# Feed-forward up projections by Strassen's seven block products

## The chip, the cores and the metric

The kernel runs on one core of a Trainium2 chip. The metric is the device time of one execution in microseconds (us), here the median of three runs. TensorE multiplies matrices, VectorE and ScalarE work elementwise, GpSimd (POOL) does small elementwise work and issues DMAs of its own, SyncE (SP) issues the weight loads.

## The reference, cut to what matters

A decoder trunk of two residual layers on 512 tokens of 1024 features, all in float32. Layer 0 mixes by block-sparse attention and spatial gating, layer 1 by gated linear attention (GLA). Each layer then attends to 256 memory tokens and ends with a SwiGLU feed-forward of width 2816:

```python
def swiglu(h, w_gu, w_down):
    g, u = jnp.split(h @ w_gu, 2, axis=-1)
    return (jax.nn.silu(g) * u) @ w_down

x = x + swiglu(rmsnorm(x, norm_ffn[l]), ffn_w_gu[l], ffn_w_down[l])
```

`w_gu` is 1024 x 5632 (gate columns first, then up columns), `w_down` is 2816 x 1024.

## The kernel before, in words

The residual stream is kept transposed: `xT` has eight tiles of 128 features x 512 tokens. Every product is done in three matmuls: each operand is split into a high part, rounded to TensorE's float32r format, and a low part, the rest (`split`, lines 99 to 105: ScalarE copies the high part, VectorE subtracts it from the source). Then high x high, high x low and low x high are added up in one PSUM bank (`mm3`, lines 126 to 129).

Weights come from HBM through SP (`load_w`, line 115) into raw buffers (two), and are split into three pairs of buffers `wh`, `wl`. `ws_tile` (line 294) makes one tile of 128 output features x 512 tokens with weights as the stationary operand. `gemm_as` (line 303) holds activations stationary and makes tiles of 128 tokens x 512 columns (matmul lines 314 to 316).

The pre-norm is folded in: `prep` (line 262) multiplies a finished tile of `xT` by the norm's gain while it splits it, and adds its squares to `acc`. `finish` (line 275) sums `acc` over the partitions on TensorE, takes the inverse root on POOL, and `rb_of` (line 231) spreads the per-token column to a row on all partitions by two matmuls. The row is applied to the products when they leave PSUM.

The feed-forward (line 885 on) works in three parts of 8, 8 and 6 hidden tiles. `ffn_hidden` makes the gate tile, scales it and applies silu, makes the up tile, scales it, multiplies both, and splits the result. The down projection of the part follows: `ws_tile` in layer 0 (`ffn_mid`), `gemm_as` in layer 1 (`ffn_last`). The tiles that feed it are made just before, in `out_last` (line 444), the last half of the cross attention's output projection, which calls `prep` for each finished tile.

SBUF beside the weights is a set of 61 slots of 128 x 512 (`Slots`, line 46; the one freed longest ago is handed out first), and small pools of their own for the softmax rows (`pp`), their transposes (`pt`), and scratch (`tj`, `em`, `es`, `acc`). PSUM has eight banks: four `m`, two `s`, two `t`.

The order of instructions on each engine is made by the framework when the program is built: among the instructions that a model of their times holds to be ready, the one that stands first in the program goes first. So an engine can take up later work while earlier work waits. On the chip each engine then runs its list strictly in that order.

Of the kernel before, what the change touches and what calls it, by code (L numbers as in the profile page):

```python
# [18 lines left out]
P = 128  # L19
# [26 lines left out]
class Slots:  # L46
    """[128, 512] fp32 slots of SBUF handed out in program order, oldest freed first."""
# [19 lines left out]
def trunk(ctx: ExitStack, tc: tile.TileContext, io, out):  # L67
# [9 lines left out]
    xp = ctx.enter_context(tc.tile_pool(name="chain", bufs=1))  # L77
# [3 lines left out]
    # ---------------------------------------------------------------- helpers  # L81
# [24 lines left out]

    def chain(tag, bufs, dtype=F32):
        return xp.tile([P, T], dtype, tag=tag, name=tag, bufs=bufs)
# [45 lines left out]
    # ---------------------------------------------------------- early loads  # L154
# [38 lines left out]
    # parameter columns  # L193
# [11 lines left out]
    # -------------------------------------------------------- x: transposes  # L205
# [25 lines left out]
    def rb_of(rcol):  # L231
        """the per-token column [128, 4] as a row on every partition [128, 512]"""
# [13 lines left out]
    def col_sums(ps, src):  # L246
        """ps[:, t] = the sums over the partitions of src's 128-token blocks"""
# [14 lines left out]
    def prep(nm, m, gcol):  # L262
        """feature tile m of the next sub-layer's input, and its part of the sum of squares"""
        h, l = split_slots(xT[m], gcol)
        nm.h.append(h)
        nm.l.append(l)
        if m == 0:
            nm.acc = tp.tile([P, T], F32, tag="acc", name="acc", bufs=1)
# [6 lines left out]
    def finish(nm):  # L275
        ps = ps_t()
        col_sums(ps, nm.acc)
        nm.rcol = rsqrt_cols(ps[:, :NT], NT, 1.0 / D)
        nm.rb = rb_of(nm.rcol)

    def new_norm():
        nm = Norm()
        nm.h, nm.l = [], []
        return nm
# [5 lines left out]
    # ------------------------------------------------------------- GEMM forms  # L290
# [3 lines left out]
    def ws_tile(wv, c0, bh, bl, k0=0):  # L294
        """one [128 features, 512 tokens] tile: weights stationary"""
# [7 lines left out]
    def gemm_as(load, ah, al, ntok, evac):  # L303
        """ntok x [128 tokens, 512 columns]: activations stationary"""
# [20 lines left out]
    # ------------------------------------------------------- memory projections  # L325
    def mem_prep(l):
        """gained and transposed memory tokens in two parts, and their norms to be applied later"""
        mh, ml, rss = [], [], []
        ss = [small(2), small(2)]
        for hf in range(2):  # L330
            r = [chain("pp", NPP), chain("pp", NPP)]
            for mt in range(2):
                nc.sync.dma_start(r[mt], io["mem"][0, mt * P:(mt + 1) * P, hf * T:(hf + 1) * T])
            for mt in range(2):
                j = tmp(tag="tj", bufs=1)
                A.activation(j, r[mt], AF.Square, accum_out=ss[mt][:, hf:hf + 1])
            for k2 in range(2):
# [11 lines left out]
                ml.append(l_)  # L349
        for mt in range(2):  # L350
# [9 lines left out]
    def kv_proj(l, mh, ml, rss):  # L360
        """keys and values of the memory; yields between its four products"""
# [7 lines left out]
        def keys(half):  # L369
            kn = [None, None]  # L370

            def evac_k(mt, ps):
                kn[mt] = sl.get()
                ss = small(2)
                for hh in range(2):
                    j = tmp(tag="tj", bufs=1)
                    A.activation(j[:, :MEM], ps[:, hh * MEM:(hh + 1) * MEM], AF.Square,
                                 accum_out=ss[:, hh:hh + 1])
                r = rsqrt_cols(ss, 2, rss[mt][1])
# [64 lines left out]
    def out_last(w, k0, ch, cl, nm, gname, l):  # L444
        """the last part, and the next sub-layer's input"""
        out_part(w, k0, ch, cl, lambda m: prep(nm, m, pcol(gname, l * KD + m)))
        finish(nm)
# [800 lines left out]
```

## Time and profile before

| | |
|---|---|
| runs (three) | median 1523.46 us, 1522.89 to 1526.95 |
| profiled execution, span | 1523.4 us |
| granted TensorE clock, mean | 0.999 |
| instructions | 18140 |
| HBM read, written | 139.88 MB, 2.10 MB |

The profile's span runs from the first to the last instruction of the profiled execution; the page gives no other time for it, and the span differs from the median of the runs by 0.06 us. In the timeline each row has a start, a duration and the instruction; matmuls overlap, so their rate is read from starts. "L128" is line 128 of the kernel before.

### The profile page before, as it was taken

To read this page: it belongs to the slowest core of one execution; us is meant where nothing else is said; L and a number is where in the kernel's file an instruction comes from. 1 tells how busy PE (TensorE), PEld (TensorE's weight loads), DVE (VectorE), ACT (ScalarE), POOL (GpSimd) and SP (SyncE) were. 2 spreads that over 40 slices of the span, in tenths; PEclk is the share of its full clock that TensorE was granted. 3 is DMA by queue.
4 is the path that set the end of the run, shared out by engine and by line. 5 is a ranking of instruction groups with operands and counts; after the bars stand their busy time and mean duration, and the time that the engine had idled before them with its cause. 6 is when DMAs were issued, how large, how long until landed. Compare 5 with 4: busy or idle time off the path is not lost.

```text
span 1523.4 us, 18140 instructions
## 1 busy us (share of the span) xinstructions
PE 1508.1 (99%) x7050; PEld 1241.8 (82%) x7050; DVE 863.9 (57%) x1451; ACT 620.2 (41%) x1014; POOL 83.3 (5%) x104
## 2 busy tenths in 40 slices
PE   8999999999999999999999999999999999999998
PEld 6787778888888888888787887888888888888887
DVE  6876875755654344344667565776557443443443
ACT  6546663643532133222454443555435332332231
POOL 4511100000000000000000000100000000000000
PEclk9999999999999999999999999999999999999999
DMA  7231432312333333333323222253123322332332
GB/s 216 83 97 56 125 102 65 97 56 97 94 89 95 102 98 94 101 95 95 103 64 97 70 69 71 94 159 93 58 68 97 97 92 91 97 95 97 97 98 95
DMA packets 197606, 143.15 MB, mean 94 GB/s; under 512 B 6093, under 2 KB 176193, under 8 KB 197521
## 3 DMA queue, kind: packets, MB, share of 16 engines
q1 hardware_dynamic: 195616, 140.53, 30.4%
q0 software_dynamic: 800, 1.37, 0.4%
q8 instruction: 55, 0.90, 0.2%
q10 hardware_dynamic: 1104, 0.11, 0.1%
q14 instruction: 31, 0.25, 0.0%
HBM read 139.88 MB, written 2.10 MB: 93 GB/s over the span
## 4 chain that ended last, share of the span: by engine, by line
PE 93%; DVE 2%; ACT 1%; POOL 1%; issue 0%; ACTq 0%; POOLq 0%
PE ps_mm L129 21%; PE ps_mm L128 21%; PE ps_mm L127 21%; PE ps_mm L314 6%; PE ps_mm L316 6%; PE ps_mm L315 6%; PE ps_t L132 2%; PE ps_s L127 1%; PE ps_t L127 1%; PE ps_t L128 1%; PE ps_t L129 1%; PE ps_s L129 1%; PE ps_s L128 1%; PE ps_s L585 1%; DVE wl L102 0%; PE ps_s L249 0%
## 5 line engine op out<-in xcount | busy, mean ns | idle before, releaser
L128 PE MATMUL ps_mm<-slot,wh 128*128 128x512 f32 x1424 | 555.9, 391 | 0.0
L129 PE MATMUL ps_mm<-slot,wl 128*128 128x512 f32 x1424 | 555.3, 391 | 0.0
L127 PE MATMUL ps_mm<-slot,wh 128*128 128x512 f32 x1424 | 552.7, 390 | 0.5 <-DVE slot L105 0.5
L101 ACT ACTIVATE wh<-raw 128x1024 fp32r<-128x1024 f32 (+1 forms) x258 | 271.6, 1053 | 631.9 <-PE ps_mm L128 469.3
L102 DVE TENSOR_TENSOR wl<-raw,wh 128x1024 fp32r<-128x1024 f32 (+1 forms) x258 | 314.1, 1218 | 161.3 <-ACT wh L101 155.0
L129 PEld LDWEIGHTS ps_mm<-slot,wl 128*128 128x128 f32 x1424 | 267.5, 188 | 55.4 <-DVE wl L102 0.2
L127 PEld LDWEIGHTS ps_mm<-slot,wh 128*128 128x128 f32 x1424 | 267.4, 188 | 55.4 <-DVE slot L105 0.6
L128 PEld LDWEIGHTS ps_mm<-slot,wh 128*128 128x128 f32 x1424 | 267.5, 188 | 54.8
L314 PE MATMUL ps_mm<-wh,slot 128*128 128x512 f32 x496 | 195.1, 396 | 1.4 <-DVE slot L711 1.4
L315 PE MATMUL ps_mm<-wh,slot 128*128 128x512 f32 x496 | 195.3, 394 | 0.0
L316 PE MATMUL ps_mm<-wl,slot 128*128 128x512 f32 x496 | 189.7, 392 | 0.0
L314 PEld LDWEIGHTS ps_mm<-wh,slot 128*128 128x128 f32 x496 | 93.7, 189 | 20.5 <-DVE slot L711 1.8
L315 PEld LDWEIGHTS ps_mm<-wh,slot 128*128 128x128 f32 x496 | 93.7, 189 | 18.3
L316 PEld LDWEIGHTS ps_mm<-wl,slot 128*128 128x128 f32 x496 | 93.2, 188 | 18.7
L898 DVE TENSOR_TENSOR tmp<-ps_mm,rb 128x512 f32<-128x512 f32 x44 | 30.4, 691 | 132.9 <-PE ps_mm L129 132.7
L139 POOL TENSOR_TENSOR s<-s,mhalf 128x2 f32<-128x2 f32 (+3 forms) x46 | 50.9, 1110 | 640.7 <-DVE s L137 636.5
L894 DVE TENSOR_TENSOR tmp<-ps_mm,rb 128x512 f32<-128x512 f32 x44 | 30.4, 691 | 94.0 <-PE ps_mm L129 90.7
L440 DVE TENSOR_TENSOR slot<-ps_mm,slot 128x512 f32<-128x512 f32 x64 | 43.5, 687 | 29.5 <-PE ps_mm L129 29.3
L914 DVE TENSOR_TENSOR slot<-ps_mm,slot 128x512 f32<-128x512 f32 x24 | 16.5, 690 | 56.9 <-PE ps_mm L129 56.9
L101 ACT ACTIVATE slot<-tmp 128x512 fp32r<-128x512 f32 x48 | 30.3, 632 | 32.6 <-DVE tmp L899 28.2
L102 DVE TENSOR_TENSOR slot<-tmp,slot 128x512 fp32r<-128x512 f32 x48 | 32.9, 685 | 2.3 <-ACT slot L101 2.1
L899 DVE TENSOR_TENSOR tmp<-tmp 128x512 f32<-128x512 f32 x44 | 30.4, 692 | 4.4 <-ACT wh L101 0.5
(285 smaller groups left out, 1362.4 us busy)
## 6 DMA issues: line engine op xcount, KB each, us to landing
raw<-in_ffn_w_gu SPq DMA_DIRECT2D x88, 512.0 KB, 3.9
raw<-in_ffn_w_down SPq DMA_DIRECT2D x38, 512.0 KB, 3.6
raw<-in_xa_w_kv SPq DMA_DIRECT2D x32, 512.0 KB, 3.8
raw<-in_od_w_in SPq DMA_DIRECT2D x24, 512.0 KB, 3.7
raw<-in_xa_w_q SPq DMA_DIRECT2D x16, 512.0 KB, 3.8
raw<-in_xa_w_out SPq DMA_DIRECT2D x16, 512.0 KB, 3.5
raw<-in_ev_w_in SPq DMA_DIRECT2D x12, 512.0 KB, 4.6
raw<-in_ev_w_in SPq DMA_DIRECT2D x16, 256.0 KB, 2.9
```

The lines of the kernel that those rows point to most:

```text
L101: A.activation(h, src, AF.Copy)
L102: V.tensor_tensor(l, src, h.bitcast(F32), ALU.subtract)
L127: PE.matmul(ps, ah, bh, start=start, stop=False)
L128: PE.matmul(ps, ah, bl, start=False, stop=False)
L129: PE.matmul(ps, al, bh, start=False, stop=stop)
L132: PE.transpose(ps, src, ident)
L139: G.tensor_tensor(r, m, mhalf[:, :n], ALU.pow)
L314: PE.matmul(pss[t], a, wh[:, kk, :], start=st, stop=False)
L315: PE.matmul(pss[t], b, wh[:, kk, :], start=False, stop=False)
L316: PE.matmul(pss[t], a, wl[:, kk, :], start=False, stop=sp_)
L440: V.tensor_tensor(xT[m], ps, xT[m], ALU.add)
L894: V.tensor_tensor(g, ps, nm.rb, ALU.mult)
```

## The change

Both operands of the up projection are cut in two along each side: tokens into halves of 256, features into even and odd tiles, columns into gate and up columns. The four block products of the result (gate and up, for each token half) are then made from seven block products in place of eight, by Winograd's form of Strassen's scheme.

- Activations: `prep7` scales a tile of `xT` by the gain on ScalarE, without a split; for each pair of tiles `blocks7` makes the four sums S1 to S4 of quarter blocks on VectorE and splits three tiles (and a fourth for each second pair).
- Weights: four products take raw blocks (A11, A12, S4, S3; for S3 one raw block is first added to another on VectorE), three take sums that are built up in slots by DMAs that add to SBUF, issued by POOL (`accum_op=ALU.add`).
- Products: activations stationary, tokens on the output's partitions, blocks of 256, then five times 512 columns of each of gate and up. Partial sums stay in PSUM where the scheme allows it, and are copied out in between.
- The norm is now a per-partition scale at the evacuation, so the row `rb` isn't made for the feed-forward norms.
- The hidden tiles, tokens on partitions, are turned by TensorE transposes (`turn`), run as `tick`s between the next block's products, and then split. The down projection takes 6, 8 and 8 tiles.
- `pp`, `pt`, `tj`, `em`, `es`, `acc` come from the slots, now 72; raw buffers are four in place of two.

The diff, cut to its core:

```diff
+    def prep7(nm, m, gcol):
+        y = sl.get((P, 2, MEM))
+        yf = y.rearrange("p a b -> p (a b)")
+        A.activation(yf, xT[m], AF.Copy, scale=gcol)
+        nm.y.append(y)
+        sum_squares(nm, m)
+        if len(nm.y) == 2:
+            blocks7(nm, *nm.y)
+            nm.y = []
+    def blocks7(nm, y0, y1):
+        first = len(nm.ops) % 2 == 0
+        e = sl.get((P, 2, MEM))
+        V.tensor_tensor(e[:, 0, :], y0[:, 1, :], y1[:, 1, :], ALU.subtract)
+        V.tensor_tensor(e[:, 1, :], e[:, 0, :], y0[:, 0, :], ALU.subtract)
+        if first:
+            nm.e4 = sl.get((P, 2, MEM))
+        V.tensor_tensor(nm.e4[:, 0 if first else 1, :], y1[:, 0, :], e[:, 1, :], ALU.add)
+        V.tensor_tensor(y0[:, 1, :], y0[:, 0, :], y0[:, 1, :], ALU.subtract)
+        h, l = [], []
+        for src in (y0, y1, e):
...
+            split(h[-1], l[-1], src)
...
+        if not first:
...
+            split(h4, l4, nm.e4)
...
-    def finish(nm):
+    def finish(nm, row=True):
...
-        nm.rb = rb_of(nm.rcol)
+        if row:
+            nm.rb = rb_of(nm.rcol)
...
+    def mm7(wv, c0, c1, w, ops, sink, tick):
...
+        for p in range(n2):
+            q.append([sl.get(), sl.get()])
+            for i in range(2):
+                k = 4 * p + 2 * i
+                nc.sync.dma_start(q[p][i][:, 0:w], wv[:, k, c1:c1 + w])
+                nc.gpsimd.dma_start(q[p][i][:, 0:w], wv[:, k, c0:c0 + w], accum_op=ALU.add)
+        pa_, pc_, pb_ = [[banks[g]() for _ in range(2)] for g in "mst"]
...
+        def chain_sum(kh=None, c=None):
+            def get(p):
+                h, l = new_hl()
+                for i in range(2):
+                    split(h[:, i, 0:w], l[:, i, 0:w], q[p][i][:, 0:w])
+                    if kh is not None:
+                        nc.gpsimd.dma_start(q[p][i][:, 0:w], wv[:, 4 * p + kh + 2 * i, c:c + w],
+                                            accum_op=ALU.add)
...
+        def steps(acc, first, get, name, end):
+            for p in range(n2):
+                h, l = get(p)
+                tick()
+                for i in range(2):
+                    oh, ol, j = ops[2 * p + i][name]
+                    st, sp_ = first and p == 0 and i == 0, p == n2 - 1 and i == 1
+                    for t in range(2):
+                        o = acc[t][:, 0:w]
+                        ah, al = oh[:, j, t * P:(t + 1) * P], ol[:, j, t * P:(t + 1) * P]
+                        PE.matmul(o, ah, h[:, i, 0:w], start=st, stop=False, skip_group_check=True)
+                        PE.matmul(o, al, h[:, i, 0:w], start=False, stop=False, skip_group_check=True)
+                        PE.matmul(o, ah, l[:, i, 0:w], start=False, stop=sp_, skip_group_check=True)
+                        if sp_:
+                            sink(end, t, o)
+                yield
...
+        product(pa_, True, raw_block(0, c0), "A11", "m")
+        product(pc_, True, chain_sum(1, c1), "S1", "q")
+        product(pb_, True, raw_block(1, c0), "A12", "b")
+        product(pa_, False, chain_sum(1, c0), "S2", "u")
+        for _ in zip(steps(pc_, False, b22, "S4", "c"), steps(pa_, False, t3, "S3", "v")):
+            pass
+        product(pa_, False, chain_sum(), "A22", "a")
...
-    parts_ff = [(0, 8), (8, 16), (16, 22)]
...
+    blocks_ff = [(0, 2), (2, 6), (6, 10), (10, 14), (14, 18), (18, 22)]
+    rounds_ff = {1: (0, 1), 3: (2, 3), 5: (4, 5)}
...
+            def sink(what, t, ps):
+                if what in ("m", "q", "u"):
+                    x = sl.get()
+                    {"m": M, "q": Q, "u": U}[what][t] = x
+                    A.activation(x[:, :w], ps, AF.Copy)
+                elif what == "b":
+                    V.tensor_tensor(M[t][:, :w], M[t][:, :w], ps, ALU.add)
+                    A.activation(M[t][:, :w], M[t][:, :w], AF.Silu, scale=nm.rcol[:, t:t + 1])
+                elif what == "c":
+                    V.tensor_tensor(U[t][:, :w], ps, U[t][:, :w], ALU.subtract)
+                    scaled(U[t][:, :w], U[t][:, :w], t, M[t][:, :w])
+                    sl.free(M[t])
+                elif what == "v":
+                    V.tensor_tensor(Q[t][:, :w], Q[t][:, :w], ps, ALU.subtract)
+                else:
+                    g = sl.get()
+                    A.activation(g[:, :w], ps, AF.Silu, scale=nm.rcol[:, 2 + t:3 + t])
+                    scaled(Q[t][:, :w], Q[t][:, :w], 2 + t, g[:, :w])
+                    sl.free(g)
...
+            def turn(j):
+                def go():
+                    ps = ps_t()
+                    for t in range(NT):
+                        transpose(ps[:, t * P:(t + 1) * P], hid[t][:, (j - j0) * P:(j - j0 + 1) * P])
+                    self.gh[j], self.gl[j] = split_slots(ps)
...
+        def rounds(self):
+            for b in range(len(blocks_ff)):
+                self.up(b)
+                if b - 1 in rounds_ff:
+                    yield self.round(*rounds_ff[b - 1])
+            sl.free(*self.nm.slots)
+            self.flush()
+            yield self.round(*rounds_ff[len(blocks_ff) - 1])
...
-NSLOTS = 61
-NPP = 4
-NPT = 7
+NSLOTS = 72
 TMP = 3
-NRAW = 2
+NRAW = 4
```

## Rows read from the trace of the kernel before

**Rows 1.** The page: busy time by engine; TensorE's granted clock in 40 slices, tenths.

```profile
PE 1508.1 (99%) x7050; PEld 1241.8 (82%) x7050; DVE 863.9 (57%) x1451; ACT 620.2 (41%) x1014; POOL 83.3 (5%) x104
...
PEclk9999999999999999999999999999999999999999
```

**Rows 2.** The page: the chain that ended last, share of the span by engine.

```profile
PE 93%; DVE 2%; ACT 1%; POOL 1%; issue 0%; ACTq 0%; POOLq 0%
```

**Rows 3.** Waits of TensorE: who for whom, us in total, times, longest.

```profile
PE ps_mm L132 <- DMA slot<-in_x: 6.0, 2, 3.5
...
PE ps_mm L127 <- DVE slot L105: 0.5, 1, 0.5
```

**Rows 4.** Timeline of TensorE (start us, duration us, instruction): two neighbours of 512 columns.

```profile
240.16 0.39 PE L128 MATMUL ps_mm<-slot,wh 128*128 128x512 f32 x1
240.38 0.39 PE L129 MATMUL ps_mm<-slot,wl 128*128 128x512 f32 x1
```

**Rows 5.** Timeline of TensorE: two neighbours of 256 columns.

```profile
337.19 0.28 PE L127 MATMUL ps_s<-slot,slot 128*128 128x256 f32 x1
337.31 0.28 PE L128 MATMUL ps_s<-slot,slot 128*128 128x256 f32 x1
```

**Rows 6.** Transposes: timeline of TensorE, and a group (count, busy us, mean ns).

```profile
1178.49 1.04 PE L132 MATMUL ps_t<-ident,slot 128*128 128x128 f32 x8
1179.28 0.48 PE L127 MATMUL ps_mm<-slot,wh 128*128 128x512 f32 x1
1179.60 0.40 PE L128 MATMUL ps_mm<-slot,wh 128*128 128x512 f32 x1
...
L132 PE MATMUL ps_t<-ident,slot 128*128 128x128 f32 x96 | 16.5, 284 | 0.0
```

**Rows 7.** Groups by line and shape: count, busy us, mean ns, idle before.

```profile
L102 DVE TENSOR_TENSOR wl<-raw,wh 128x1024 fp32r<-128x1024 f32 x250 | 306.6, 1226 | 160.2 <-ACT wh L101 153.9 <-PE ps_mm L128 5.6
L101 ACT ACTIVATE wh<-raw 128x1024 fp32r<-128x1024 f32 x250 | 264.9, 1060 | 613.7 <-PE ps_mm L128 453.1 <-PE ps_mm L315 111.2 <-issue 21.7
L102 DVE TENSOR_TENSOR slot<-tmp,slot 128x512 fp32r<-128x512 f32 x48 | 32.9, 685 | 2.3 <-ACT slot L101 2.1
L101 ACT ACTIVATE slot<-tmp 128x512 fp32r<-128x512 f32 x48 | 30.3, 632 | 32.6 <-DVE tmp L899 28.2 <-DVE tmp L733 4.4
L102 DVE TENSOR_TENSOR sL<-st,sH 128x256 fp32r<-128x256 f32 x28 | 11.7, 421 | 5.8 <-ACT sH L101 5.4 <-PE ps_s L129 0.2
```

**Rows 8.** Timeline of VectorE in layer 0's last half of the attention's output projection.

```profile
383.08 1.29 DVE L440 TENSOR_TENSOR slot<-ps_mm,slot 128x512 f32<-128x512 f32 x2 [5.02 <-PE ps_mm L129]
...
397.18 0.69 DVE L440 TENSOR_TENSOR slot<-ps_mm,slot 128x512 f32<-128x512 f32 x1
...
400.17 0.69 DVE L273 TENSOR_TENSOR acc<-acc,tmp 128x512 f32<-128x512 f32 x1
400.78 0.75 DVE L105 SCALAR_TENSOR_TENSOR slot<-slot,pc,slot 128x512 fp32r<-128x512 f32 x1
401.44 0.69 DVE L273 TENSOR_TENSOR acc<-acc,tmp 128x512 f32<-128x512 f32 x1
```

**Rows 9.** Windows: length, busy by engine (instructions), granted clock, DMA share, GB/s.

```profile
0.00:38.00 38.00, 30.52 (x134) 25.22 (x135) 24.67 (x77) 23.67 (x50) 15.48 (x33) 1.00 0.72 216
...
382.00:404.00 22.00, 22.00 (x99) 18.23 (x98) 19.02 (x27) 13.21 (x20) 0.00 (x0) 1.00 0.33 96
...
420.00:460.00 40.00, 40.00 (x178) 33.12 (x177) 21.08 (x26) 14.18 (x18) 0.00 (x0) 1.00 0.32 92
...
960.00:963.40 3.40, 3.40 (x16) 2.95 (x17) 1.63 (x4) 0.49 (x2) 0.00 (x0) 0.51 0.02 8
```

**Rows 10.** DMA issues: tile, queue, count, KB each, median us to landing.

```profile
raw<-in_ev_w_in SPq DMA_DIRECT2D x16, 256.0 KB, 2.9
...
slot<-in_ev_w_s POOLq DMA_DIRECT2D x2, 256.0 KB, 6.6
```

**Rows 11.** Timeline of POOL: one issue of a DMA of 256 KB.

```profile
13.10 0.56 POOL L653 DMA_DIRECT2D slot<-in_ev_ln_g  x1
```

More of the change, by code (lines that the diff above doesn't have):

```diff
@@ L283, in new_norm @@
         nm.h, nm.l = [], []
+        nm.y, nm.ops, nm.slots = [], [], []
         return nm
@@ L323, in as_loader, with block, load, new_hl @@
         return load
+    def mm7(wv, c0, c1, w, ops, sink, tick):
+        n2 = len(ops) // 2
+        def block(kh, c, p):
+            return wv[:, 4 * p + kh:4 * p + kh + 3:2, c:c + w]
+        def load(kh, c, p):
+            raw = wp.tile([P, 2, T], F32, tag="raw", name="raw", bufs=NRAW)
+            nc.sync.dma_start(raw[:, :, 0:w], block(kh, c, p))
+            return raw
+        def new_hl():
+            return (wp.tile([P, 2, T], F32R, tag="wh", name="wh", bufs=NWH),
+                    wp.tile([P, 2, T], F32R, tag="wl", name="wl", bufs=NWL))
+        q = []
+        for p in range(n2):
[5 more added lines that the diff above has]
+        pa_, pc_, pb_ = [[banks[g]() for _ in range(2)] for g in "mst"]
+        def raw_block(kh, c):
+            def get(p):
+                raw = load(kh, c, p)
+                h, l = new_hl()
+                split(h[:, :, 0:w], l[:, :, 0:w], raw[:, :, 0:w])
+                return h, l
+            return get
+        def chain_sum(kh=None, c=None):
+            def get(p):
+                h, l = new_hl()
+                for i in range(2):
[3 more added lines that the diff above has]
+                                            accum_op=ALU.add)
+                if kh is None:
+                    sl.free(*q[p])
+                return h, l
+            return get
+        def t3(p):
+            r = load(0, c1, p)
+            V.tensor_tensor(r[:, :, 0:w], r[:, :, 0:w], r22[p][:, :, 0:w], ALU.add)
+            h, l = new_hl()
+            split(h[:, :, 0:w], l[:, :, 0:w], r[:, :, 0:w])
+            return h, l
+        r22 = {}
+        def b22(p):
+            r22[p] = load(1, c1, p)
+            h, l = new_hl()
+            split(h[:, :, 0:w], l[:, :, 0:w], r22[p][:, :, 0:w])
+            return h, l
+        def steps(acc, first, get, name, end):
+            for p in range(n2):
+                h, l = get(p)
+                tick()
+                for i in range(2):
+                    oh, ol, j = ops[2 * p + i][name]
[9 more added lines that the diff above has]
+                yield
+        def product(*args):
+            for _ in steps(*args):
+                pass
[4 more added lines that the diff above has]
+        for _ in zip(steps(pc_, False, b22, "S4", "c"), steps(pa_, False, t3, "S3", "v")):
+            pass
+        product(pa_, False, chain_sum(), "A22", "a")
@@ L330, in mem_prep @@
         for hf in range(2):
[L331 removed]
+            r = [sl.get(), sl.get()]
             for mt in range(2):
@@ L349, in mem_prep @@
                 ml.append(l_)
+            sl.free(*r)
         for mt in range(2):
@@ L442, in out_part, with out_last @@
                     done(m)
-    def out_last(w, k0, ch, cl, nm, gname, l):
-        out_part(w, k0, ch, cl, lambda m: prep(nm, m, pcol(gname, l * KD + m)))
-        finish(nm)
+    def out_last(w, k0, ch, cl, nm, gname, l, seven=False):
+        make = prep7 if seven else prep
+        out_part(w, k0, ch, cl, lambda m: make(nm, m, pcol(gname, l * KD + m)))
+        finish(nm, not seven)
     wv = wview(io["ev_w_in"][0])
@@ L627, in moba_pair @@
             split(oH, oL, osum)
+            sl.free(osum)
             sl.free(qH, qL, kH, kL)
@@ L864, in cross @@
                 ptl.append(l_)
+            sl.free(*pts)
             for dv in range(2):
@@ L872, in cross @@
                 oL.append(l_)
+            sl.free(*pth)
+            sl.free(*ptl)
         sl.free(*kh)
@@ L923, in ffn_last @@
         xk = None
-        for pi, (j0, j1) in enumerate(parts_ff):
-            gh, gl = ffn_hidden(l, nm, j0, j1)
-            last = pi == len(parts_ff) - 1
-            if last:
-                free_norm(nm)
+        for j0, gh, gl, last in Ffn(l, nm).rounds():
             if xk is None:
@@ L1070, in gla_qk @@
         ksH, ksL = split_slots(ps)
+        sl.free(em, es)
         hs[hd] = ep, qpH, qpL, kiH, kiL, ksH, ksL
```

97 lines of the change are left out of this document (61 added, 36 removed).

## The prediction, made before the changed kernel ran

> **What bounds the kernel now.** I read the busy shares first: TensorE is busy 99% of a span of 1523.4 us and its clock is at full level in every slice [rows 1]. The chain of waits agrees: 93% of it is TensorE [rows 2]. The list of TensorE's waits shows that it hardly waits behind its first loads: the input transposes wait 6.0 us for x, and no product on the feature tiles of a norm loses more than 0.5 us to VectorE, over the whole run [rows 3]. So the time is a count of TensorE instructions times their spacing, and everything else is cover. The spacing is read from starts, not from the durations, which overlap: matmuls of 512 columns start 0.227 us apart [rows 4], of 256 columns 0.120 us apart [rows 5]. The profile's span (1523.4) and the median of the runs (1523.46) differ by 0.06 us, so the sum below is made against 1523.4 and holds for both.
>
> **The up projections.** Before, each layer makes 44 tiles of 8 x 3 matmuls of 512 columns: 1056 x 0.2267 = 239.4 us. After, a block makes 7 products, each of 4 feature tiles x 2 token halves x 3 = 24 matmuls: 168. Five blocks are 512 wide, 5 x 168 x 0.2267 = 190.4 us, one is 256 wide, 168 x 0.120 = 20.2 us. Per layer 28.8 us go, for both **-57.6 us**. It is the pattern of the activations-stationary loops, whose neighbours have the same spacing, so I take no range on it.
>
> **The turns.** The output stands with tokens on partitions and must be turned: 22 x 4 = 88 transposes a layer, 176 in all. Eight of them in the trace hold TensorE from 1178.49 to 1179.28 us, 0.10 each, and the matmul behind them starts its successor 0.09 late [rows 6]. A group of four is then about 0.46 us (0.35 to 0.5), 44 groups: **+20.2 us** (15 to 22). The Trainium skill speaks against this edit (TensorE: Matmul & The Clock Gate, Part 4: PE-mode transpose): it puts a 128x128 transpose inside a kernel at some 275 ns. Rows 6 have that number as the mean duration (284 ns), but not as the spacing; by the page the edit would cost 48 us, by the spacing 20 us. I sum with the spacing.
>
> **The row of norms.** The feed-forward norms no longer spread rcol to a row: two 512-column matmuls in each layer go, **-0.9 us**; the ScalarE and VectorE steps of that row lay beside TensorE anyway.
>
> **The start of the feed-forward.** This is the price I expect to see most. While TensorE makes the last half of the attention's output projection, VectorE already runs without a gap from 383.08 to 402.1 us [rows 8], 19.0 us busy in 22 [rows 9]. TensorE's own last tile there was ready at 397.2, its split for the norm at 401.5; TensorE bridged that without a wait, since the feed-forward's first output tiles need it last. After, VectorE loses eight scaled subtractions (start to start 0.66: 5.3 us) and gains 16 half-size differences (0.42 us each, back to back some 0.34: 5.4 us) and 14 split halves of 128x512 (0.69, back to back 0.60: 8.4 us) [rows 7, 8]. So its work ends 8.5 us later, at about 410.6; the first product needs all but the last three splits, 408.8. TensorE can put in between only what needs feature tiles 0 to 3 and has weight buffers (three pairs): the first half of the products A11 and S1 in the narrow block, 24 x 0.120 = 2.9 us, and 0.8 us of column sums. Idle: 408.8 - 397.2 - 3.7 = 7.9 us. After idle time the trace shows the clock at its lower level (1.2 GHz, granted 0.51) for 3.4 us [rows 9], which takes half of that again, 1.7 us. 9.6 us a layer: **+19.2 us**. Ends: 6 us if the scheduler slips the weight splits and more half-products into the gaps, 28 us if VectorE takes everything in program order and the ScalarE halves add waits.
>
> **Inside a block.** Per wide block TensorE has 38.1 + 1.8 = 39.9 us. VectorE has eight 128x1024 splits (1.23), two additions of that size, twelve 128x512 splits (0.69), ten evacuation steps and four splits of turned tiles (0.69): 30.2 us, 76%; ScalarE 8 x 1.06 + 22 x 0.63 + the silus = 25 us [rows 7]. Before it was 21.1 us in 40 [rows 9]. That fits on average, with three weight buffer pairs of 2.7 us each ahead. One wait has no cover: the subtraction of the S3 partial sum (label v) reads the bank on which A22, the very next product, accumulates. The first bank is read 0.69 us while the second bank's last three matmuls run (0.68); the pipeline's end (0.39 - 0.23 = 0.16) and the semaphores leave 0.3 us bare. When VectorE is just in another instruction (it is 70% of the time, half of 0.7 to 1.2 us left) another 0.3 comes on top. 0.6 x 12 blocks: **+7.2 us**, between 0 (next block's matmuls fill it) and 24 (each time a whole 1.23 us split and a second one stand before). What is queued behind: the c steps and A22's own splits, all with slack of one product, 5.4 us.
>
> **The narrow block** gives every wait half the cover: **+2 us** for both layers, from 0 to 6.
>
> **The summing DMAs.** T sums are made by DMAs that add to SBUF, 12 a block, issued by POOL (0.56 us each, and POOL has nothing else there) [rows 11]. None is in the trace. The nearest row is a plain 256 KB load from POOL, 6.6 us to landing in the crowded start, against 2.9 us from SP [rows 10]. The slack: S1's first split can begin when its buffer is freed, at A11's start; it is done 2.3 us later, the DMA goes out, and S2 wants its own split to begin 14.3 us after A11's start (six half-products of 2.72, less 2.0): 12 us. At 3 to 6.6 us it is hidden, also if reading the destination makes it half as long again: +0, between 0 and 48 (landing in 16 us). Bytes: a wide block moves 8.4 MB in 39.9 us, 210 GB/s; the first 38 us of the kernel moved 216 GB/s at a DMA share of 0.72 [rows 9]. SP's loads will therefore land later than now, but four raw buffers instead of two cover that: 0.
>
> **Pooled buffers.** Attention and GLA take their scratch from the common slots. Counted through, at least ten slots are free at the tightest place of the feed-forward, and a slot comes back several products after it was freed: 0, between -3 and +3 (these stages lose little to waits now, and could gain or lose it).
>
> **Sum.** -57.6 + 20.2 - 0.9 + 19.2 + 7.2 + 2 = -9.9: 1523.4 - 9.9 = **1513.5 us**.
>
> **The rivals.** Without any wait the arithmetic alone gives 1523.4 - 38.3 = 1485.1 us.
> (a) The preparation is hidden and the v wait filled: 1485.1 + 3 = 1488. For it: the order of work already fills such places (0.5 us of waiting at most at the old starts). Against: VectorE's work there exceeds TensorE's, and no order makes it less. 0.18.
> (b) The start costs its upper end, 28 us: 1522. 0.12.
> (c) VectorE's order inside the blocks fails: 2 us a block and 6 for the narrow ones, 1485.1 + 19.2 + 24 + 6 = 1534. Speaking for it: peaks, since in A22's 5.4 us VectorE has 6.9 us; against: three buffers ahead. 0.10.
> (d) The slower side: the adding DMA lands late. S2's split waits for it, TensorE stands at S2 in every block. From 12 us of landing on each further us costs 10 us over the wide blocks, so from about 13 us the change is a loss; at 16 us, 4 us x 12 = 48: 1561. For it: 6.6 us for a plain one, and this one reads its target too; against: that row is from the crowded start. 0.12.
> (e) The transposes cost their duration, not their spacing: 176 x 0.284 = 50 us instead of 20.2: 1543. The page named above would have it so. Rows 6 speak against it. 0.04.
> My forecast has 0.44.
>
> **How the numbers follow.** A measurement of this kernel tells about 0.3%, 4.6 us, from no change: below 1518.9 is faster, above 1528.0 slower. Faster: (a) and nearly all of the forecast, 0.60. Same: (b) and the edges, 0.16. Slower: (c), (d) and (e), less an edge, 0.24. The range leaves out half of (d) and (e) above and the tail of (a): 1486 to 1538; the forecast's own range is 1503 to 1524.
>
> **What would show it.** TensorE idle of some 8 us with the clock halved behind it at both feed-forward starts, released by VectorE splits of prep; 2016 up matmuls with unchanged spacing; groups of four transposes at 0.4 to 0.5 us; a wait of 0.3 to 1 us on the v subtraction once a block; adding DMAs landing in under 8 us and no TensorE wait behind them. I am wrong if the starts cost under 3 us each, if the blocks are spaced above 42 us, or if the S2 splits wait for DMA.

## The result, and the profile after

The changed kernel takes 1576.08 us (median of 4 runs, 1567.11 to 1580.58), the kernel before, beside it, 1523.18 (1522.29 to 1526.95): ratio 1.0328, 95% interval [1.0293, 1.0363]. It is slower by 53 us where I said 10 faster, and outside the range. The profiled execution has a span of 1578.9 us, 55.5 more than before. In each run here an execution's time is some 1.7 us longer than its span (1580.58 and 1578.9), so the 0.06 us between span and median before was chance.

The page of the changed kernel: busy time, tenths in 40 slices, DMA queues (packets, MB, share of 16 engines) and the chain by engine.

```profile
PE 1510.9 (96%) x7126; PEld 1237.6 (78%) x7126; DVE 974.0 (62%) x1651; ACT 737.8 (47%) x1258; POOL 211.0 (13%) x248
...
PEclk9999889999999999999999999999999999999999
DMA  8222313313579378436322212263146774773351
...
q1 hardware_dynamic: 137120, 152.07, 30.6%
q0 software_dynamic: 21536, 35.98, 14.0%
...
PE 83%; DVE 4%; DMA 4%; ACT 3%; issue 1%; POOL 1%; DVEq 0%; ACTq 0%; POOLq 0%
```

The count of instructions is the predicted one: 7050 [rows 1] - 96 up matmuls - 4 of the norm rows + 176 transposes = 7126. But TensorE's part of the chain fell from 93% [rows 2] to 83%, and DMA, VectorE and ScalarE have taken the rest. The DMA line reaches 9 tenths in the first feed-forward and 7 in the second.

TensorE's waits, longest first (the same view as [rows 3]: us in total, times, longest), and VectorE's longest wait for a DMA.

```profile
PE ps_t L443 <- DVE slot L101: 17.4, 4, 7.6
PE ps_mm L443 <- ACT wh L100: 9.9, 8, 3.2
PE ps_mm L128 <- DMA slot<-in_x: 5.4, 2, 3.6
PE ps_s L444 <- DVE slot L101: 5.1, 2, 2.7
PE ps_mm L444 <- DVE slot L101: 4.6, 2, 2.3
```

```profile
DVE raw L420 <- DMA raw<-in_ffn_w_gu: 54.0, 18, 7.8
```

L443 to L445 are the three matmuls of a product, L101 is the low half of a split, L420 the addition that makes S3's weight sum. ps_t is the pair of PSUM banks that A12's product and the turned hidden tiles use in turn. The place of the longest wait, in layer 0, on the chain (start us, us; the first line, a group of four transposes, is used further down), on VectorE's timeline, on TensorE's, and in windows (length, busy of PE, PEld, DVE, ACT, POOL, granted clock, DMA share, GB/s):

```profile
573.36 0.44 PE ps_t L128 x4
...
623.87 10.48 DMA raw<-in_ffn_w_gu
634.70 0.88 issue
635.58 0.69 DVE slot L101
636.32 0.80 PE ps_t L443
```

```profile
625.91 0.69 DVE L101 TENSOR_TENSOR wl<-slot,wh 128x512 fp32r<-128x512 f32 x1
634.44 1.23 DVE L420 TENSOR_TENSOR raw<-raw 128x1024 f32<-128x1024 f32 x1 [7.83 <-DMA raw<-in_ffn_w_gu]
635.58 1.28 DVE L101 TENSOR_TENSOR slot<-ps_t,slot 128x512 fp32r<-128x512 f32 x2
```

```profile
628.05 0.62 PE L445 MATMUL ps_mm<-wl,slot 128*128 128x512 f32 x2
636.32 0.80 PE L443 MATMUL ps_t<-wh,slot 128*128 128x512 f32 x1 [7.65 <-DVE slot L101]
636.91 0.63 PE L444 MATMUL ps_t<-wh,slot 128*128 128x512 f32 x1
637.34 0.63 PE L445 MATMUL ps_t<-wl,slot 128*128 128x512 f32 x1
```

```profile
620.00:630.00 10.00, 8.67 (x42) 6.51 (x40) 5.04 (x6) 7.26 (x12) 4.79 (x6) 1.00 1.06 204
630.00:640.00 10.00, 3.68 (x9) 2.91 (x10) 3.62 (x5) 0.63 (x1) 1.75 (x2) 0.67 0.53 113
```

Read them together. The DMA engines are full (share 1.06) and a raw block for S3 takes 10.48 us. VectorE has its addition next in order and stands for 7.83 us, with the splits of two turned tiles behind it. Those tiles keep the ps_t banks, so A12's first matmul stands for 7.65 us, though it has nothing to do with S3. The matmuls after it start 0.43 us apart instead of 0.227 [rows 4]: after the idle time TensorE's clock is at its lower level (1.2 GHz; granted 0.67 in the mean of the window).

The account by stage. A stage ends here where the next norm's column sums begin on TensorE's timeline; us. Each row is one execution, and the runs of the changed kernel lie 13 us apart, so a few us between rows or between cures tell nothing.

| kernel (spans) | even mixer | cross 0 | FFN 0 | gated layer | cross 1 | FFN 1 | span |
|---|---|---|---|---|---|---|---|
| before | 290.9 | 116.5 | 357.9 | 280.6 | 119.9 | 357.6 | 1523.4 |
| after | 303.1 | 120.5 | 379.9 | 287.0 | 120.9 | 367.5 | 1578.9 |
| pools only | 302.8 | 119.9 | 358.1 | 282.6 | 119.9 | 357.7 | 1541.1 |
| 76 slots, 2 raw | 297.7 | 119.9 | 358.1 | 289.5 | 119.9 | 357.6 | 1542.8 |
| turns' own banks | 304.5 | 120.5 | 369.5 | 284.3 | 120.9 | 362.5 | 1562.1 |
| GpSimd's sums | 302.5 | 119.9 | 359.0 | 282.7 | 119.9 | 357.9 | 1541.8 |
| both of these | 304.0 | 119.7 | 356.7 | 284.3 | 119.7 | 356.1 | 1540.5 |
| both, own scratch, 3 raw | 304.4 | 118.6 | 360.6 | 282.8 | 120.9 | 358.1 | 1545.5 |
| both, own scratch, 2 + 1 raw | 310.8 | 118.6 | 371.2 | 285.2 | 120.9 | 368.6 | 1575.3 |
| before, tj and es moved | 300.8 | 116.5 | 357.9 | 286.0 | 119.9 | 357.7 | 1538.6 |
| before, the same and 3 raw | 298.3 | 116.5 | 357.9 | 287.0 | 119.9 | 357.6 | 1537.2 |

Stages that the change was not about lose 23.5 us (12.2 + 4.0 + 6.3 + 1.0), the feed-forwards 32 (22.0 + 9.9). The pitch is the spacing of TensorE's instructions when nothing waits; it alone fell by 19.9 us a layer. So waits in the feed-forwards are 39.8 + 32 = 72 us. A sum of how much farther apart the matmuls start than their pitch places them: 29 at the two starts (the preparation and the narrow block) and 45 inside the other blocks, to within 2 us.

### The profile page after: what moved, and what is told of

The parts are those of the page before. It is cut to its first block, busy times and chain, and to the rows that moved or that the text cites. A ratio compares the mean times of both kernels' runs of the same rounds, so it can differ in the third digit from the quotient of the medians.

```text
span 1578.9 us, 19243 instructions
## 1 busy us (share of the span) xinstructions
PE 1510.9 (96%) x7126; PEld 1237.6 (78%) x7126; DVE 974.0 (62%) x1651; ACT 737.8 (47%) x1258; POOL 211.0 (13%) x248
## 3 DMA queue, kind: packets, MB, share of 16 engines
q1 hardware_dynamic: 137120, 152.07, 30.6%
q0 software_dynamic: 21536, 35.98, 14.0%
HBM read 186.02 MB, written 2.10 MB: 119 GB/s over the span
## 4 chain that ended last, share of the span: by engine, by line
PE 83%; DVE 4%; DMA 4%; ACT 3%; issue 1%; POOL 1%; DVEq 0%; ACTq 0%; POOLq 0%
PE ps_mm L123 10%; PE ps_mm L124 10%; PE ps_mm L125 10%; PE ps_mm L355 6%; PE ps_mm L356 6%; PE ps_mm L357 6%; PE ps_mm L443 5%; PE ps_mm L444 5%; PE ps_mm L445 4%; DMA raw<-in_ffn_w_gu 3%; PE ps_t L128 2%; PE ps_s L444 2%; PE ps_s L443 2%; PE ps_s L445 2%; ACT wh L100 2%
## 5 line engine op out<-in xcount | busy, mean ns | idle before, releaser
L100 ACT ACTIVATE wh<-raw 128x1024 fp32r<-128x1024 f32 (+2 forms) x266 | 272.4, 1025 | 369.5 <-PE ps_mm L124 175.5
L101 DVE TENSOR_TENSOR wl<-raw,wh 128x1024 fp32r<-128x1024 f32 (+2 forms) x266 | 315.0, 1187 | 180.0 <-ACT wh L100 175.0
L123 PE MATMUL ps_mm<-slot,wh 128*128 128x512 f32 x720 | 282.7, 396 | 3.9 <-ACT wh L100 2.1
L124 PE MATMUL ps_mm<-slot,wh 128*128 128x512 f32 x720 | 284.4, 395 | 0.0
L125 PE MATMUL ps_mm<-slot,wl 128*128 128x512 f32 x720 | 283.1, 395 | 0.0
L123 PEld LDWEIGHTS ps_mm<-slot,wh 128*128 128x128 f32 x720 | 136.6, 190 | 34.3 <-ACT wh L100 4.3
L124 PEld LDWEIGHTS ps_mm<-slot,wh 128*128 128x128 f32 x720 | 136.6, 190 | 27.5
L125 PEld LDWEIGHTS ps_mm<-slot,wl 128*128 128x128 f32 x720 | 136.6, 190 | 27.3
L443 PE MATMUL ps_mm<-wh,slot 128*128 128x512 f32 (+1 forms) x384 | 147.7, 388 | 10.0 <-ACT wh L100 9.9
L444 PE MATMUL ps_mm<-wh,slot 128*128 128x512 f32 (+1 forms) x384 | 145.8, 381 | 4.6 <-DVE slot L101 4.6
L445 PE MATMUL ps_mm<-wl,slot 128*128 128x512 f32 (+1 forms) x384 | 136.6, 378 | 0.0
L411 POOL DMA_DIRECT2D slot<-in_ffn_w_gu x96 | 86.9, 1151 | 350.4 <-DVE wl L101 334.2
L101 DVE TENSOR_TENSOR wl<-slot,wh 128x512 fp32r<-128x512 f32 (+1 forms) x144 | 88.3, 643 | 33.2 <-ACT wh L100 32.0
L443 PEld LDWEIGHTS ps_mm<-wh,slot 128*128 128x128 f32 x384 | 73.4, 193 | 25.7 <-ACT wh L100 13.1
```

The source lines that it names most:

```text
L100: A.activation(h, src, AF.Copy)
L101: V.tensor_tensor(l, src, h.bitcast(F32), ALU.subtract)
L123: PE.matmul(ps, ah, bh, start=start, stop=False)
L124: PE.matmul(ps, ah, bl, start=False, stop=False)
L125: PE.matmul(ps, al, bh, start=False, stop=stop)
L411: nc.gpsimd.dma_start(q[p][i][:, 0:w], wv[:, 4 * p + kh + 2 * i, c:c + w], accum_op=ALU.add)
```

## The experiments

Lines left out are marked; medians beside the kernel before, which took 1525.1 to 1525.6 in these runs. The first four ran together.

**The pools alone**: the old feed-forward with the pooled scratch.

```
-NSLOTS = 61; NPP = 4; NPT = 7; NRAW = 2
+NSLOTS = 72; NRAW = 4      # pp, pt, tj, em, es, acc from the slots
...                         # feed-forward as before
```

> The old feed-forward, with the scratch of attention and GLA taken from 72 common slots and four raw buffers, as in the change. In the changed kernel the stages outside the feed-forward are longer by 12.2 (even mixer), 4.0 and 1.0 (cross attention), 6.3 us (GLA), 23.5 in all. Theory: the pooling makes them so: 1523 + 23 = 1546 us (1540 to 1552). Rival: the pooling is free and these stages suffer from something that the new feed-forward brings (another order, loads queued before it): 1523 us, 3 either way.

1543.42 us, ratio 1.0122 [1.0105, 1.0138]: 18 us, of which the table has 11.9 in the even mixer, 3.4 in the first cross attention and 2.0 in the gated layer. "Pooled buffers: 0" is refuted, for the pools and the four raw buffers together.

**The adding DMAs**, left out (S1, S2 and A22 then use a raw block in place of their sums), or overwriting instead of adding (the sums are left out there too; same bytes, same queue).

```
-nc.gpsimd.dma_start(q[p][i][:, 0:w], wv[...], accum_op=ALU.add)
+nc.gpsimd.dma_start(q[p][i][:, 0:w], wv[...])        # second run; first run: no line; both places
```

> The changed kernel with its 144 adding DMAs left out (the weight sums are then only their first block). Theory: these DMAs fill the DMA engines, raw loads land 5 to 10 us late, and VectorE, in order, stands at the addition for S3 behind such a load; without them the waits inside the blocks (45 us) go, and some 8 us at the starts: 1576 - 53 = 1523 us (1518 to 1533). Rival: VectorE's and ScalarE's own work is too much for the blocks, whatever the DMAs do: over 1560 us.

> The changed kernel with the same 144 DMAs from POOL as plain loads that overwrite (the weight sums are then only their last block): same bytes from HBM, same waits, no reading of the target. If the adding itself is dear (these DMAs took 98 us of one engine per MB in the changed kernel, all SP loads 51): about half of the 53 us comes back, 1545 to 1555 us. Rival, the bytes alone do it: 1570 us or more.

1550.81 (1.0170 [1.0153, 1.0188]) and 1552.05 (1.0176 [1.0161, 1.0191]). Half of what I expected of the first run came back: by the count above its blocks still wait for about 24 us of the 45. The same bytes without adding are as good as no bytes at all: the adding is dear, not the traffic. From the run that overwrites, the line of GpSimd's queue and VectorE's wait in front of S3's addition; then the issues (count, KB, us to landing) of the changed kernel and of that run:

```profile
q0 software_dynamic: 11552, 35.98, 7.3%
...
DVE raw L419 <- DMA raw<-in_ffn_w_gu: 25.7, 15, 3.8
```

```profile
raw<-in_ffn_w_gu SPq DMA_DIRECT2D x80, 512.0 KB, 4.9
slot<-in_ffn_w_gu POOLq DMA_DIRECT2D x120, 256.0 KB, 5.9
```

```profile
raw<-in_ffn_w_gu SPq DMA_DIRECT2D x80, 512.0 KB, 3.8
slot<-in_ffn_w_gu POOLq DMA_DIRECT2D x120, 256.0 KB, 3.9
```

The same 35.98 MB take 14.0% of 16 engines when they add and 7.3% when they don't: 0.140 x 16 x 1578.9 / 35.98 = 98 us of one engine for a MB against 50. The adding DMAs also go in twice as many packets (21536 against 11552). That alone is not what is dear: SP's loads, with smaller packets still (137120 for 152.07 MB), take 51 us for a MB. The raw loads beside the adding DMAs land in 4.9 us against 3.8, and VectorE waits 54.0 us for them against 25.7. The Trainium skill (DMA: Bandwidth & Descriptors, Issuing engines are not separate DMA queues) says that transfers issued by different engines share the same 16 DMA engines. The landings of the raw loads agree, since what GpSimd's queue does more shows as later landings of SP's.

**S3's addition** left out (S3 then uses the plain block).

```
-V.tensor_tensor(r[:, :, 0:w], r[:, :, 0:w], r22[p][:, :, 0:w], ALU.add)
```

> The changed kernel without VectorE's addition for S3's weights (S3 then takes a raw block). Theory that the place of this addition at the head of VectorE's queue is what carries the late loads to TensorE: the turned tiles' and the sums' splits are no longer held up, 1540 to 1555 us. Rival: the late load holds up the split of the same block anyway, on ScalarE and VectorE: 1565 us or more.

1549.86 (1.0158 [1.0143, 1.0173]). It takes 24 instructions of at most 1.2 us off an engine that is 62% busy and gives back 26 us: what cost was VectorE standing in order behind a late load, not its work. The loads are hardly less late than in the changed kernel:

```profile
raw<-in_ffn_w_gu SPq DMA_DIRECT2D x80, 512.0 KB, 4.5
```

Leaving the addition out could also free S4's raw block sooner. But SP's issues of these loads wait for VectorE's splits as long as before (367.7 us against 366.7), so that is not the gain.

**Turned tiles in banks of their own**, in the ps_mm pair that no product holds.

```
-ps = ps_t()
+ps = turn_banks[j % 2]
```

> The changed kernel, with the turned hidden tiles in two PSUM banks of their own (the two of the four that no product holds) in place of the two that A12's product also uses. Theory 'shared banks': A12's first matmul waits until VectorE has split the last turned tiles; 17.4 us of TensorE's idle time stand in front of it in the changed kernel, and they go in part: 1558 to 1568. Rival 'the banks are only where the late loads are seen': TensorE stands a little later for the same late addition on VectorE, 1573 to 1578.

1556.18 (1.0200 [1.0183, 1.0217]), 20 us back, a little more than I gave it. The wait in front of A12 is gone from TensorE's list, though VectorE waits for the same loads as before:

```profile
DVE raw L423 <- DMA raw<-in_ffn_w_gu: 51.3, 18, 8.1
```

**GpSimd's sums.** No adding DMA; raw blocks are added by GpSimd, S4 goes beside S2, S3's sum is a difference.

```
+G.tensor_tensor(q[p][i][:, 0:w], q[p][i][:, 0:w], raw[:, i, 0:w], ALU.add)
...
+G.tensor_tensor(r[:, i, 0:w], q[p][i][:, 0:w], r[:, i, 0:w], ALU.subtract)
```

> The changed kernel without adding DMAs: the sums over the weight blocks are added by GpSimd from raw blocks (S4's product goes beside S2's, S3's sum is taken as a difference from the chain). Loads fall from 16 to 12 MB a block and none of them adds. Theory 'adding DMAs are what makes the loads late, and VectorE's in-order addition carries it to TensorE': 1548 to 1555, as without them or without that addition. Rival 'the sums themselves are late, whoever makes them' (16 additions of 1024 columns a block at 2.6 to 4.4 us on GpSimd, 42 to 70 us of a block's 57): 1570 or more.

1543.98 (1.0125 [1.0110, 1.0140]): 32 us back, better than expected. (The 16 and 12 MB of the expectation are twice too much: HBM reads fall from 186.02 to 162.95 MB in all, some 2 MB a block.) The waiting for raw blocks now stands on GpSimd, behind which no tile of another product is queued:

```profile
POOL slot L398 <- DMA raw<-in_ffn_w_gu: 192.9, 29, 29.6
```

The feed-forward stages are now as long as before. With **both** edits, these sums and the turned tiles' own banks:

> The sums added by GpSimd from raw blocks (1544 alone) and, with it, the turned tiles in two PSUM banks of their own (20 us alone, on the changed kernel). Theory 'the turned tiles wait for VectorE mostly because a late load holds VectorE': with the loads on time little is left in front of A12 (0.4 to 0.9 us twice or thrice a layer), 1537 to 1542. Rival 'the two costs add': 1544 - 20 = 1524.

1541.46 (1.0105 [1.0091, 1.0119]), 2.5 us better where the own banks alone gave 20. So the costs do not add. They are links of one chain: adding DMA, late load, VectorE in order, unsplit turned tile, bank, A12. Cutting one link gave back 20 us (the bank), 24 and 25 (the adding) and 26 (VectorE's addition). GpSimd's sums take out the adding and VectorE's addition together and gave 32, all three 35; the single gains would add up to some 70.

Even so nothing is won. By the same count 22 us at the two starts and 14 inside the blocks are left of the waits, and the other stages of this kernel are 20 us longer than before; together that is more than the 39.8 us of the pitch. At the starts TensorE still waits for VectorE's splits of the preparation (this kernel):

```profile
PE ps_mm L446 <- DVE slot L101: 4.6, 2, 2.3
PE ps_s L446 <- DVE slot L101: 3.8, 2, 2.0
```

**The start.** Two attempts on the changed kernel: three operations of the preparation moved to GpSimd; the sum of squares moved into the first block.

```
-V.tensor_tensor(nm.acc, nm.acc, sq, ALU.add)
+G.tensor_tensor(nm.acc, nm.acc, sq, ALU.add)         # and e4's sum, y0's difference
```

```
+self.todo += [squares2(m) for m in range(0, KD, 2)] + [lambda: finish(nm, False)]
```

> The changed kernel, with three of the preparation's operations ahead of the feed-forward moved from VectorE to GpSimd, which idles there: the sum of squares' additions, the fourth sum's additions and the differences for the third sum. By the rows VectorE loses 0.69 + 2 x 0.42 us a feature tile pair half, about 9 us of work in each layer. Theory 'VectorE is what the start waits for': the two starts lose 29 us of TensorE's spacing together and get back 8 to 14: 1562 to 1568. Rival 'the chain through the pair's four blocks sets it, and GpSimd is slower per tile (1.3 us an addition of 512 columns)': 1574 to 1584.

> The changed kernel with only the sum of squares of the feed-forward's input moved into the first block. Theory 'the start waits for VectorE's queue' (28.8 us of excess in both starts, part of which is the late adding DMAs): 1565 to 1571. Rival 'the late adding DMAs set the start': 1574 to 1578.

1590.14 (1.0428 [1.0411, 1.0445]), 14 us worse, and 1577.43 (1.0327 [1.0307, 1.0347]), no change. GpSimd's additions, from the groups of the first run (count, busy us, mean ns, idle before):

```profile
L272 POOL TENSOR_TENSOR slot<-slot,tmp 128x512 f32<-128x512 f32 x14 | 24.0, 1716 | 2.8 <-ACT tmp L271 2.5
```

1.72 us where VectorE takes 0.69, in order with the adding DMAs' issues: the column sums of layer 0 came 8.9 us later than in the changed kernel (432.5 against 423.6). The 1.3 us of the expectation is a multiplication of this size; the addition beside it in the kernel before takes 2.2. The Trainium skill (GPSIMD Engine Reference, Engine selection) calls such work on GpSimd about half as fast as VectorE. This trace has 2.5 times, beside a busy VectorE. The second edit did not do what it says: on the built kernel's timeline the additions still stand among the preparation's splits, because the framework takes up what is ready. VectorE's load at the start is thus not taken away by either, and what it is worth alone stays open.

**What the pools cost.** Four more slots, two raw buffers; then the stages' own scratch again, with three and with two raw buffers, on the kernel with both good edits.

> The pooled buffers with the old feed-forward, as in the run with the pools alone (1543), but with 76 slots and two raw buffers in place of 72 and four; the memory taken is the same. Theory 'too few slots': in the attention of the even mixer only 2 of 72 slots are free at the narrowest, so a tile waits for the reading of one that was freed a moment ago; with four more the 12 us lost there come back for the most part: 1526 to 1533. Rival 'handing out oldest-freed-first costs by itself', however many there are: 1540 to 1546. Rival 'four raw buffers let the loads and splits run ahead into the attention': that too would give 1526 to 1533, and the place of the gain in the trace has to tell the two apart.

> The kernel with GpSimd's sums and the turned tiles' own banks, and the scratch tiles of the attention stages and the gated layer taken back from the common slots: 61 slots, four and seven chain tiles in rotation as before, three raw buffers, the feed-forward's own scratch in the chain tiles' room. Theory 'pooling costs by itself': the 18 us that the pools alone cost come back, 1519 to 1526, the even mixer ends at 291 to 293 and the cross stages take 116 and 120. Rival 'the third raw buffer or the loads' running ahead is what shifts the mixers': the even mixer stays above 297, 1533 or more.

> The kernel with GpSimd's sums, turned tiles' own banks and the stages' own scratch (1549.8), but with two raw buffers for the mixers and projections; the third is used by the up projections alone. Theory 'the order, set by the raw buffers': the even mixer comes back to 291 to 293 and the kernel to 1532 to 1538. Rival 'what moved the mixers is something else in the change': the even mixer stays at 298 or more, 1545 to 1552.

1544.30 (1.0136 [1.0113, 1.0160]), 1549.82 (1.0158 [1.0145, 1.0172]), 1572.94 (1.0303 [1.0278, 1.0329]). None of my three theories (slots, handing out, raw buffers) was borne out. Four more slots and two raw buffers fewer halve the even mixer's loss (297.7), and the gated layer loses it again (289.5); with its own scratch and two raw buffers the mixer is worst (310.8). The feed-forward hints at what raw buffers are worth there: 356.7 us with four, 360.6 with three, 371.2 where the up projections have three and the others two of them. It is no clean price, since the feed-forward's scratch and the order of the buffers differ as well. So I turned to the kernel before, with a smaller step: only the single tiles tj and es taken from the pt rotation, without and with a third raw buffer.

```
-tmp(tag="tj", bufs=1)   ...   tmp(tag="es", bufs=1)
+chain("pt", NPT)        ...   chain("pt", NPT)
+NRAW = 3                                             # second run only
```

> The same as the run with a third raw buffer, but with the two of before: es and tj from the pt rotation alone. Both theories: within 4 us of before, 1522 to 1529; if it is slower by more, the two scratch tiles have a share in what the third raw buffer seems to cost.

> The kernel before with a third raw buffer, and nothing else but that two single scratch tiles (es, tj) are taken from the pt rotation to make room. Theory 'the order': how many raw and scratch buffers there are goes into the order in which the framework lays each engine's instructions; with a third one the value and output products run ahead of the even mixer's attention and leave nothing between its heads, whose transposes then wait for VectorE: the even mixer ends at 300 to 304, 1534 to 1540. Rival 'only the handing out of common slots does that': 291, 1523 to 1527.

1537.38 (1.0077 [1.0063, 1.0091]) and 1539.31 (1.0080 [1.0064, 1.0096]). The control, for which both theories said nothing would happen, is the finding: moving two scratch tiles into the pt rotation costs 12 us without any common slots. In the profiled execution, which took 15 us more, 9.9 are in the even mixer and 5.4 in the gated layer. TensorE in 181 to 198 us (length, busy, granted clock, DMA share, GB/s), of before, of the control, of the pools alone:

```profile
181.00:198.00 17.00, 16.12 (x86) 1.00 0.19 59
```

```profile
181.00:198.00 17.00, 13.92 (x58) 0.67 0.10 34
```

```profile
181.00:198.00 17.00, 12.33 (x50) 0.75 0.12 38
```

And TensorE's timeline there, of before (large products come from 188.75 on) and of the control (nothing but small matmuls of the heads and transposes until 197.94):

```profile
188.38 0.61 PE L132 MATMUL ps_mm<-ident,slot 128*128 128x128 f32 x4
188.75 0.48 PE L314 MATMUL ps_mm<-wh,slot 128*128 128x512 f32 x1
189.06 0.40 PE L315 MATMUL ps_mm<-wh,slot 128*128 128x512 f32 x1
```

```profile
183.04 1.41 PE L132 MATMUL ps_t<-ident,pp 128*128 128x128 f32 x6 [0.94 <-DVE em L626]
185.43 0.80 PE L622 MATMUL ps_t<-pt,slot 128*128 128x512 f32 x1 [0.98 <-DVE pt L102]
...
191.13 1.44 PE L132 MATMUL ps_mm<-ident,slot 128*128 128x128 f32 x8 [0.87 <-DVE slot L105]
...
197.94 0.78 PE L314 MATMUL ps_mm<-wh,slot 128*128 128x512 f32 x1
```

TensorE's list is another one in the control. Up to this place both kernels have issued the same large products. Before, 50 small matmuls follow, the heads' own woven with the turning of queries and keys, and then large products again; in the control 64 small ones stand in a row, a second head's in front of the turning. There TensorE waits for VectorE three times by 0.9 us, and its clock is at the lower level for the greater part of the stretch. Six transposes take 1.41 us, and 0.82 elsewhere at the full clock. The idle time is the small part: 3.1 of the 17 us, which have a granted clock of 0.67 in the mean. By the count of spacings 9 of the mixer's 10 us lie between 170 and 200 us. No idle time in this stretch, of TensorE, VectorE or ScalarE, is ended by the release of a moved tile.

If the order is the cause, another written-out order should cure it with every buffer left as it is. I put keys' and values' products between the attention's pairs, on the kernel with both good edits and on the kernel before.

```
-ORDER = "... a0 q1 a1 free k k t1m a2 a3 k k k k out"
+ORDER = "... a0 q1 a1 free k k k k t1m a2 k k a3 out"
-GLA_ORDER = "... free S3 out mem k k k k k k"
+GLA_ORDER = "... free mem k S3 k k k k k out"
```

> The kernel with GpSimd's sums and the turned tiles' own banks (1541.5), with another order written out for the even mixer (keys' and values' products k k k k between a1 and t1m, k k between a2 and a3, instead of k k and, behind a3, k k k k) and for the gated layer (the memory's preparation and one product ahead of S3, out last). Theory 'order': what the pools cost is lost where TensorE's list has no large products between the attention's small ones; in the new list the longest such stretch of the even mixer falls from 8.8 us of matmuls to 3.4 (4.4 in the kernel before). The even mixer ends at 288 to 294 instead of 304: 1524 to 1531. Rival 'waits on common slots': they stay, the mixer ends at 300 or later, 1538 or more.

> The kernel before with the same two written-out orders and nothing else. No theory needs it to move far: its longest stretch of small matmuls in the even mixer is 4.2 us as before (4.4): 1520 to 1530. If the order was tuned to the old buffers alone it is slower by 5 or more; if it is better for both, the gain of the run beside it is not due to the seven products.

1549.07 (1.0157 [1.0142, 1.0172]) and 1541.90 (1.0112 [1.0095, 1.0129]). No cure: the mixer ends at 310.6, where I had put the rival, and on the kernel before the new order costs 17 us, so it is worse for either kernel. Shown is that the even mixer and the gated layer lose time to each of these disturbances (the mixer 6 to 20 us, the gated layer 2 to 10), of buffers or of the written order, and that in the control the mixer's loss sits where small dependent matmuls stand alone, for the most part at the lower clock. That the framework's order, rather than a wait on common or moved buffers, is what passes it on fits the timelines of the control, but was not shown by a cure. No version tried beats the kernel before; the best is the one with both good edits, 1.0105 of it.

Two further runs, the deferred squares (1548.26) and the first block's sums by adding DMAs (1572.55), were within 2 us of the kernels they were made from and tell nothing apart.

## Why the prediction was wrong, step by step

- **What bounds the kernel** held, and so did the arithmetic: instruction count exact, pitch -19.9 us a layer against -19.2 predicted (57.6 - 20.2 + 0.9, halved). The transposes cost their spacing: four of them 0.44 us on the chain, with a mean duration of 0.27. Rival (e) falls: the 275 ns of the Trainium skill (TensorE: Matmul & The Clock Gate, Part 4: PE-mode transpose) are a duration here too, not the price.
- **The start**: +19.2 predicted with +2 for the narrow block, 29 measured. The mechanism was right in part. VectorE runs from 398.77 without a gap to 427, where I had 410.6 on the old time axis, 426 with the 15.7 us by which the stage began later. TensorE waits for its splits of the preparation 9.7 us in the two layers (the rows with `slot L101` on ps_s and ps_mm above), where I had 15.8; from 420 to 430 us its granted clock is 0.66. Part of the rest is late adding DMAs, which I had at nothing: without them the starts lose 22. In layer 0 one of them stands on the chain at the end of the narrow block, where the slack is half as long. ScalarE, in order, waits behind it, and TensorE then for ScalarE, 3.2 us (start and duration of the adding DMA; ScalarE's waits for adding DMAs in the whole run):

```profile
435.04 8.64 DMA slot<-in_ffn_w_gu
...
ACT wh L100 <- DMA slot<-in_ffn_w_gu: 5.7, 5, 2.4
```

- **Inside a block**: +7.2 predicted for the v subtraction, which shows no such wait (with both good edits it shows three times, 2.0 us in all). 45 us measured, at another place: A12's first matmul, and ScalarE's and VectorE's splits. The step that failed was to look for waits on the accumulating bank and not on the bank that is shared with the turns. Rival (c), VectorE's order inside the blocks, came nearest in kind, with less than the size: 24 + 6.
- **The summing DMAs**: this step failed most. I asked when an adding DMA lands and not what it takes from the others. The landing was right: 5.9 us, at most 11.6, inside the 12 us of slack. TensorE does not stand at S2 in every block, so rival (d) as told did not happen; splits of the sums wait for an adding DMA five times, 5.7 us in all (the row above). That SP's loads will land later but four raw buffers cover it, "0", is the wrong term: with plain DMAs of the same size 24 us come back. My own figures had the warning, 210 GB/s wanted against 216 moved in the crowded start, and I priced the adding at no engine time. And I had listed the third sum's addition among VectorE's work without asking what stands behind it when its load is late.
- **Pooled buffers: 0, between -3 and +3**: measured +18, with the four raw buffers. I counted free slots at the tightest place of the feed-forward; the loss is in the mixers, and four more slots with two raw buffers fewer did not bring it back (1544.30). I took stages with few waits as safe. As I read it now, few waits were the sign of an order that had no slack to give; that is not shown, and the cause of this term stays open.
- Sum by measured terms: -39.8 + 29 + 45 + 23.5 = 57.7, against 55.5 of span; 2 us of start are counted in cross 0 as well.

## What to carry to other kernels

Price a DMA that adds by the engine time it takes from the loads beside it, not only by when it lands; and for each instruction on an in-order engine that waits for a load, ask which unrelated tiles and banks are released behind it. Do not cost a re-pooling of buffers at zero where a framework lays the order of instructions: here moving two scratch tiles cost 12 us, so measure the re-pooling alone first. When several single cures give the same gain, suspect one chain, and count the gain once.

## What the runs showed of the hardware that I had not expected

- An adding DMA from HBM into SBUF takes 98 us of one DMA engine for a MB, a plain one on the same queue 50, SP's loads 51 (30.6% x 16 x 1578.9 / 152.07).
- GpSimd's issue of an adding DMA takes 1.15 us in the mean, of a plain one 0.54 in the otherwise equal run. Issues can overlap: 96 adding ones hold GpSimd for 86.9 us, 96 plain ones for 51.4.
- The granted clock was 0.67 over 17 us in which TensorE stood still for 3.1 us in all, in gaps of at most 1 us between small matmuls. In the kernel before it was 1.00 in the same window, with 0.9 us of standing still and large products in the second half.
